# Cached window rows through on-chip slots in the last layer, and five smaller edits to a planned hybrid trunk kernel

## The chip, the cores and the metric

One core of a Trainium2 chip runs the whole program in one launch. Time is device microseconds of that core, lower is better. The kernel before takes 2428.99 us (median of 3 runs, 2427.99 to 2431.45).

## The reference

One inference step through four layers, A (gated short convolution), B (native sparse attention), C (RG-LRU recurrence) and A again, for 1024 prompt tokens and 8 x 4 sample tokens, width 1024, in f32. Beside the two results it returns new states; one of them is the sliding-window cache of the samples, a plain shift of the old one by four rows.

```python
def short_conv_mixer(x, buf, w_in, conv_w, w_out):
    h, b_gate, c_gate, z = jnp.split(x @ w_in, 4, axis=-1)
    conv, new_buf = causal_dwconv(c_gate * h, buf, conv_w)
    return (jax.nn.silu(z) * b_gate * conv) @ w_out, new_buf
...
x <- LayerNorm(ALPHA * x + mixer(x))
...
# nsa_win_sample: (8 samples, 512 rows, k and v, 2 heads, 64)
win = jnp.concatenate([win_buf, win_new], axis=1)   # the last 512 rows are returned
```

So rows 4 to 511 of each sample's cache, 508 rows of 1 KB (520,192 bytes), are returned unchanged as rows 0 to 507, and only the last four rows are computed (in layer B).

## The kernel before

Tokens lie in the free dimension, features in partitions: 1056 tokens as three pieces of 352 (`TC`), 1024 features as eight tiles of 128. A product in f32 is three products of split halves (`split` makes a high part by a cast on ScalarE and a low part by a subtraction on VectorE or GpSimd), so one piece of one output tile is a group of 24 matmuls in `dense`, and one weight tile (512 KB, loaded into `ws`, split into `w`) serves three such groups.

Every call is recorded (`Rec`), not issued: `Rec.lay` then plays a list schedule with a cost for each operation, a bus for the transfers and due times, over rings of tile slots (`big` 18 slots of 8.25 KB, `w` 3, `ws` 4 or 5, `c` 8 or 9 of one piece each, PSUM `mm` 5 and `aux` 3), and the order that it finds is the order on TensorE, VectorE, ScalarE and GpSimd. All instructions so recorded have line L310. The order of the transfers on SP, the queue that issues nearly all of them, is set by the framework beneath; SP issues them one by one, each when what it waits for is there, and each also waits for the transfer eight before it.

The first A layer carries side work (`compress`): 64 gathers of 1 MB of the paged cache by GpSimd, summed on GpSimd and VectorE, and written back to DRAM as `raw` (128 stores). It is shared over the layer's 96 steps (`share`): `RATE` side steps for each step. What remains is done at the layer's end. After the side work the layer's last carried rows `SC` are transposed on TensorE and stored.

In layer A a step (w, j) is a weight tile and a piece. For output tile c = 0 the pieces are outermost (three weights for j = 0, then for j = 1, then j = 2), so that the layer can begin while the LayerNorm of the layer before is still at work on the later pieces; that LayerNorm reloads what it needs by `c<-xc` and `c<-dd`. From c = 1 on each weight serves its three pieces in a row.

The old window rows are copied from DRAM to DRAM by eight transfers written in layer C (`gate_out`, one for each c). Nothing that they read depends on the program before them.

In layer B (`b_project`) the tiles of keys and values leave PSUM by a ScalarE copy into a slot of ring `c` (`kv`), one for each of 9 token tiles, from which rows are stored and keys transposed (`put_k`). `kl1` holds the low parts of the keys of group 1, by a transfer.

Stages of the profiled execution, in us from the span's start: first layer A 0 to 414, its output product to 540, projections of B to 690, sample attention to 861, prompt attention to 1455, output of B to 1560, C to 1850 and its output to 1935, the last A 1947 to 2301, its output to the end.

Of the kernel before, what the change touches and what calls it, by code (L numbers as in the profile page):

```python
# [240 lines left out]
class Rec:  # L241
# [136 lines left out]
    def lay(self):  # L378
        ops = self.ops
        for o in ops:  # L380
            o.weak -= o.deps
            o.left, o.ready, o.outs, o.follow = len(o.deps) + len(o.weak), 0.0, [], []
        for o in ops:
            for d in o.deps:
                d.outs.append(o)
            for d in o.weak:
                d.follow.append(o)
        free = {e: 0.0 for e in self.ENGINES}
        pend = {e: [] for e in self.ENGINES}
        able = {e: [] for e in self.ENGINES}  # L390
        num = {id(o): i for i, o in enumerate(ops)}
        parked = {}
        for r in self.rings:
            r.next = 0
            r.free = [0.0] * (r.n - len(r.held))
            for t in r.held:
                if not t.keep and not t.left:
                    r.free.append(0.0)

        def admit(o):  # L400

            for t in o.takes:
                if t.ring.next != t.seq or not t.ring.free:
                    parked[id(t.ring), t.seq] = o
                    return
            for t in o.takes:
                r = t.ring
                r.free.sort()
                o.ready = max(o.ready, r.free.pop(0))
                r.next += 1  # L410
            heapq.heappush(pend[o.eng], (o.ready, num[id(o)], o))
            for t in o.takes:
                wake(t.ring)

        def wake(r):
            o = parked.get((id(r), r.next))
            if o is not None and r.free:
                del parked[id(r), r.next]
                admit(o)
        for o in ops:  # L420
            if not o.left:
                admit(o)
        order, bus, table = [], 0.0, None
        while True:
            best = None
            for e in self.ENGINES:
                if able[e]:
                    s = free[e]
                elif pend[e]:
                    s = max(free[e], pend[e][0][0])  # L430
                else:
                    continue
                if best is None or s < best[0]:
                    best = (s, e)
            if best is None:
                break
            s, e = best
            while pend[e] and pend[e][0][0] <= s:
                _, i, o = heapq.heappop(pend[e])
                heapq.heappush(able[e], (o.due, i, o))  # L440
            o = heapq.heappop(able[e])[2]
            cost = o.cost
            if o.func is not None:
                f = o.func == AF.Sqrt
                if table is not f:
                    cost += 1283
                table = f
            if e == "SP":
                free[e] = s + 100
                bus = max(bus, s + 100) + o.size / 360  # L450
                o.end = bus + 2000
            else:
                free[e] = o.end = s + cost
                if o.size:
                    bus = max(bus, o.end) + o.size / 360
                    o.end = bus + 2000
            order.append(o)
            o.start = s
            for k in o.follow:
                k.ready = max(k.ready, s + .01)  # L460
                k.left -= 1
                if not k.left:
                    admit(k)
            for k in o.outs:
                lat = 0 if o.size and e == "POOL" else self.LAT.get((e, k.eng), 100)
                k.ready = max(k.ready, o.end + lat)
                k.left -= 1
                if not k.left:
                    admit(k)
            for t in o.tiles:  # L470
                t.left -= 1
                t.end = max(t.end, o.end + 150)
                if not t.left and not t.keep:
                    t.ring.free.append(t.end)
                    wake(t.ring)
        if len(order) != len(ops):
            done = {id(o) for o in order}
            stuck = [(o.eng, o.due, [t.name for t in o.takes], [t.ring.tag for t in o.takes]) for o in ops if id(o) not in done]
            raise RuntimeError(f"{len(stuck)} steps cannot start: {stuck[:12]}")
        return order  # L480
# [18 lines left out]
class Trunk:  # L499
# [447 lines left out]
    def layer_a(self, pm, a, X, lp, side=None, nxt=()):  # L947
        nc, io = self.nc, self.io
        stt = nc.vector.scalar_tensor_tensor
        win = io["a_w_in"][a]  # L950
        U = [None] * NCH
        SC = lp.tile([P, NCH, 36 if self.later else 18], F32, name="SC")
        todo = [(w, c) for c in range(NCH) for w in (0, 2, 3, 1)]
        wkey = lambda x: ("a", a) + x
# [12 lines left out]
        for c in range(NCH):  # L967
            g = self.wsl(1074)
# [5 lines left out]
            def step(w, j):  # L974
# [7 lines left out]
                if w == 0:  # L982
                    hs[j] = self.ct(TC)
                    nc.scalar.copy(hs[j], ps)
                elif w == 2:
                    nc.vector.tensor_mul(g[:, 2 + j * TC:2 + j * TC + np_], ps[:, 0:np_], hs[j][:, 0:np_])
                    if j == 2:
                        nc.vector.tensor_mul(gs[:, :, 2:6], ps[:, 320:352].rearrange("p (b t) -> p b t", t=4),
                                             hs[j][:, 320:352].rearrange("p (b t) -> p b t", t=4))
                elif w == 3:  # L990
                    th[j] = self.ct(TC)
                    nc.scalar.activation(th[j], ps, AF.Tanh, scale=0.5)
                    stt(out=th[j], in0=th[j], scalar=1.0, in1=ps, op0=ALU.add, op1=ALU.mult)
                else:
                    u = th[j]
                    stt(out=u, in0=ps, scalar=0.5, in1=u, op0=ALU.mult, op1=ALU.mult)
                    n = TC if j < 2 else 368
                    cv = self.aux(pm)[:, 0:n]
                    o = j * TC
                    nc.scalar.activation(cv, g[:, o:o + n], AF.Copy, scale=self.par(c, R_CA + 3 * a))  # L1000
                    for k in (1, 2):
                        stt(out=cv, in0=g[:, o + k:o + k + n], scalar=self.par(c, R_CA + 3 * a + k), in1=cv, op0=ALU.mult, op1=ALU.add)
                    parts = [(0, np_, cv[:, 0:np_])]
                    if j == 2:
                        parts.append((320, 352, cv[:, 320:368].rearrange("p (b t) -> p b t", t=6)[:, :, 2:6]))
                    for a0, b0, v in parts:
                        uv, uh, ul = u[:, a0:b0], *(U[c][:, i, o + a0:o + b0] for i in range(2))
                        if a0:
                            uv, uh, ul = (q.rearrange("p (b t) -> p b t", t=4) for q in (uv, uh, ul))
                        nc.vector.tensor_mul(v, uv, v)  # L1010
                        self.split(uh, ul, v, "act", "dve")
            U[c] = self.view2(self.big(F32R))
            if c == 0:
                seq = [(w, j) for j in range(3) for w in (0, 2, 3)] + [(1, j) for j in range(3)]
# [63 lines left out]
    def layer_c(self, pm, X, lp):  # L1078
        nc, io = self.nc, self.io
# [103 lines left out]
        def gate_out(c):  # L1183
            h2, i = H[c // 2], c % 2
# [3 lines left out]
            for j in range(3):  # L1188
# [5 lines left out]
                stt(out=th, in0=th, scalar=1.0, in1=ps, op0=ALU.add, op1=ALU.mult)  # L1194
                stt(out=th, in0=th, scalar=0.5, in1=h2[:, i, sl], op0=ALU.mult, op1=ALU.mult, wk=[("z", c)])
                self.split(u[:, 0, sl], u[:, 1, sl], th, "act", "pool")

            nc.sync.dma_start(win_s[c, 0:508, :], cache[c, 4:512, :], rk=[("z", c)])
        UC, GT, WA, H = {}, {}, {}, {}
        win_s = io["o_nsa_win_sample"][0].rearrange("b t c g d -> b t (c g d)")  # L1200
        cache = io["cache_nsa_win"][0].rearrange("b t c g d -> b t (c g d)")
        for x in ORDER_C.split():
            c = int(x[1])
            if x[0] == "u":
# [170 lines left out]
    def b_project(self, pm, X, bs, ds):  # L1375
        nc, io = self.nc, self.io
# [24 lines left out]
        def put_k(br, ps, g0, n):  # L1401


            for g in range(2):
                kd = K[br]
                r0, r1 = slice(64 * g, 64 * g + 64), slice(64 - 64 * g, 128 - 64 * g)
                sl = slice(g0, g0 + n)
# [10 lines left out]
        for half in range(2):  # L1418
# [8 lines left out]
            for g4 in ((0, 1, 2) if half == 0 else (2, 0, 1)):  # L1427
                tts = range(4 * g4, min(4 * g4 + 4, 9))
                kn = []
                if half == 1 and g4 == 0:  # L1430
                    side = self.decode_prepare(pm, q2, self.decode_gates(pm, GS, ds), KN, VN, ds)
                for tt in tts:
# [7 lines left out]
                            nc.tensor.matmul(ps, a, b, start=n == 0, stop=n == 23)  # L1440
                            n += 1
                    next(side, None)
                    kv = self.ct(nw)
                    if half == 0:
                        nc.scalar.copy(kv, ps)
                    else:
# [759 lines left out]
FOFF = 7  # L2206
OUT0, OUTD, OUT1, OUTE = 119.07, 2.4, 114, 0.993
OUTS = ((0, 0), (0, 1), (1, 0), (1, 1))
RATE = 0.7
GAHEAD = 3  # L2210
ORDER_C = "u101 u001 u12 u02 u2 g0 u5 z0 u3 g1 u4 g2 z1 z2 g3 u6 g4 u7 g5 z4 z3 g6 z6 z5 g7 z7"
NLO = (((2, 5, 6, 7), (3, 4, 6), (0, 5)), ((6, 7), (0, 5, 7), (2, 7)), ((2, 4, 6, 7), (1, 2, 6), (0, 1, 2, 3, 6, 7)))
# [14 lines left out]
TAILV = 39  # L2227
VLO = 0b10010010
SEL0 = 1
SELT = (3, 9, 18)  # L2230
DSH = dict(sel=7.1, kin=-11.8, begin=-11.6, keys=2.2, score=-10.9, turn=30.4, pv=-26.1, vin=-88.9, first=-37.1, vals=-23.0,
       fin=17.8, fold=-41.1, weights=-59.0, exps=-96.3)
DN = 3, 3, 3, 1
# [189 lines left out]
```

## Time and profile before

| | before |
|---|---|
| median of 3 runs | 2428.99 us |
| the profiled execution's own time | 2425.75 us |
| its span | 2423.7 us |
| TensorE busy in the span | 2305.6 us (95%) |
| VectorE, ScalarE, GpSimd busy | 1583.6, 1203.7, 959.3 us |
| bytes moved | 320.34 MB, 132 GB/s over the span |

TensorE is the long engine. A time is predicted against the profiled execution's own 2425.75 us; the median lies 3.24 us above that. An engine's idle time is read with what ended it, and a transfer engine's load with the DMA share of a stretch, which is the mean over the core's 16 DMA engines.

### The profile page before, as it was taken

How to read it: one execution, taken by the hardware profiler on the slowest of the kernel's cores; microseconds unless marked ns; L12 is line 12 of the kernel's file. 1: busy time of each engine (PE TensorE's matmuls, PEld its weight loads, DVE VectorE, ACT ScalarE, POOL GpSimd, SP SyncE). 2: the span in 40 equal slices, each digit the busy share in tenths (PEclk: the TensorE clock that was granted, in tenths of full speed). 3: DMA queues.
4: the chain of work that ended last, by engine and by line, in shares of the span. 5: the costliest groups of instructions: out<-in, count | busy, mean ns of one | idle time of the engine just before them, and what ended most of it. 6: DMA issues, size and time to landing. Idle time of an engine off the chain costs nothing. (4 is left out here: it accounts for less than half of the span.)

```text
span 2423.7 us, 41400 instructions
## 1 busy us (share of the span) xinstructions
PE 2305.6 (95%) x14801; PEld 2234.8 (92%) x14801; DVE 1583.6 (65%) x3686; ACT 1203.7 (50%) x2757; POOL 959.3 (40%) x1070
## 2 busy tenths in 40 slices
PE   8999997997989989999999999989999999999996
PEld 8999997996888879999999989989999999999996
DVE  5786875575358877777777777787765753433336
ACT  3211111234438878888888883487863442222233
POOL 3454543213137765565555552333463320000131
PEclk9999999997999999999999999999999999999998
DMA  7999988347356752111111234331113321111112
GB/s 260 351 350 338 321 291 281 98 151 245 104 175 230 247 201 56 33 47 43 47 48 41 78 123 124 117 103 53 53 47 118 99 67 53 44 44 53 35 46 72
DMA packets 334642, 320.34 MB, mean 132 GB/s; under 512 B 19462, under 2 KB 301542, under 8 KB 324964
## 3 DMA queue, kind: packets, MB, share of 16 engines
q1 hardware_dynamic: 325220, 250.58, 33.4%
q0 software_dynamic: 9216, 67.11, 7.4%
q8 instruction: 117, 1.92, 0.3%
q14 instruction: 89, 0.73, 0.1%
HBM read 237.31 MB, written 84.48 MB: 133 GB/s over the span
## 5 line engine op out<-in xcount | busy, mean ns | idle before, releaser
L310 PE MATMUL mm<-x,w 128*128 128x352 f32 x5760 | 948.9, 326 | 29.6 <-DVE ws L310 10.3
L310 PEld LDWEIGHTS mm<-x,w 128*128 128x128 f32 x5760 | 936.4, 190 | 36.6 <-DVE w L310 7.6
L310 PE MATMUL mm<-big,w 128*128 128x352 f32 x2208 | 375.4, 325 | 1.0 <-ACT c L310 1.0
L310 PEld LDWEIGHTS mm<-big,w 128*128 128x128 f32 x2208 | 357.2, 189 | 2.8 <-ACT c L310 1.3
L310 POOL TENSOR_TENSOR w<-ws,w 128x1024 fp32r<-128x1024 f32 (+1 forms) x43 | 104.8, 2438 | 445.8 <-ACT w L310 426.7
L1968 DVE TENSOR_TENSOR c<-T,c 128x512 fp32r<-128x512 f32 (+1 forms) x320 | 204.7, 648 | 49.3 <-ACT c L1964 44.9
L1964 ACT CAST c<-T 128x512 fp32r<-128x512 f32 (+1 forms) x320 | 174.3, 551 | 59.3 <-PE T L1960 37.7
L310 ACT CAST w<-ws 128x1024 fp32r<-128x1024 f32 (+2 forms) x116 | 120.3, 1038 | 163.3 <-PE mm L310 119.4
L641 PE MATMUL D<-x,w 128*128 128x352 f32 x1008 | 195.5, 330 | 2.2 <-DVE big L2095 2.2
L1870 PE MATMUL A<-big 128*128 128x320 f32 (+11 forms) x832 | 181.5, 334 | 3.4 <-DVE ast L1895 1.6
L1975 PE MATMUL O<-c,big 128*128 128x256 f32 x1056 | 180.4, 291 | 0.5 <-ACT c L1964 0.2
L310 POOL TENSOR_TENSOR big<-big,ws 128x1024 f32<-128x1024 f32 (+1 forms) x38 | 89.6, 2358 | 199.0 <-DMA big<-in_cache_nsa_kv,idx 103.9
L641 PEld LDWEIGHTS D<-x,w 128*128 128x128 f32 x1008 | 159.8, 188 | 5.7 <-DVE big L2095 3.5
L310 DVE TENSOR_TENSOR big<-big 128x256 f32<-128x256 f32 (+3 forms) x204 | 150.5, 758 | 21.7 <-POOL big L310 20.3
L310 DVE TENSOR_TENSOR w<-ws,w 128x1024 fp32r<-128x1024 f32 (+2 forms) x73 | 93.9, 1286 | 105.6 <-ACT w L310 104.8
L310 ACT CAST big<-aux 128x352 fp32r<-128x352 f32 (+3 forms) x116 | 45.4, 399 | 229.9 <-DVE aux L310 160.6
L1975 PEld LDWEIGHTS O<-c,big 128*128 128x128 f32 x1056 | 147.2, 189 | 2.5 <-DVE c L1968 0.7
L1928 POOL TENSOR_SCALAR pr<-pr,G,ast 128x32 f32<-128x32 f32 (+6 forms) x192 | 125.6, 668 | 47.1 <-DVE ast L1939 41.3
L1870 PEld LDWEIGHTS A<-big 128*128 128x128 f32 x832 | 134.3, 193 | 10.0 <-PE A L1870 2.2
L310 ACT ACTIVATE aux<-ws,PT 128x352 f32<-128x352 f32 (+2 forms) x72 | 42.7, 593 | 172.5 <-DVE ws L310 167.9
L1924 ACT ACTIVATE pr<-pr,ast 128x32 f32<-128x32 f32 (+6 forms) x192 | 118.4, 619 | 18.3 <-DVE ast L1895 17.4
L310 DVE SCALAR_TENSOR_TENSOR c<-c,mm 128x352 f32<-128x352 f32 x125 | 64.1, 515 | 92.3 <-ACT c L310 54.6
(286 smaller groups left out, 4032.7 us busy)
## 6 DMA issues: line engine op xcount, KB each, us to landing
ws<-in_a_w_in SPq DMA_DIRECT2D x64, 512.0 KB
raw<-big SPq DMA_DIRECT2D x128, 256.0 KB
big<-raw SPq DMA_DIRECT2D x128, 256.0 KB
c<-dd SPq DMA_DIRECT2D x48, 176.0 KB
xs<-x SPq DMA_DIRECT2D x24, 352.0 KB
x<-xs SPq DMA_DIRECT2D x8, 1056.0 KB
ws<-in_a_w_out SPq DMA_DIRECT2D x16, 512.0 KB
ws<-in_c_w_in SPq DMA_DIRECT2D x16, 512.0 KB
```

What stands on the lines that cost most here:

```text
L310: getattr(real, name)(*[f(x) for x in a], **{q: f(x) for q, x in k.items()})
L641: self.nc.tensor.matmul(ps, a, b, start=n == 0, stop=n == 23 and last)
L1870: nc.tensor.matmul(o, q[:, hl, i * P:(i + 1) * P], k, start=m == 0, stop=m == 1)
L1924: nc.scalar.activation(S[:, a:a + m], S[:, a:a + m], AF.Exp, bias=st[:, k:k + 1], scale=-1.0, accum_out=st[:, 3 + k:4 + k])
L1928: nc.gpsimd.tensor_scalar(S[:, a:a + m], S[:, a:a + m], G[:, i, 16 * k + h:16 * k + h + 1], st[:, 6 + k:7 + k], op0=ALU.mult, op1=ALU.mult)
L1964: nc.scalar.copy(x["H"][:, 0:n], x["tp"][:, 0:n])
L1968: nc.vector.tensor_sub(x["L"][:, 0:n], x["tp"][:, 0:n], x["H"][:, 0:n].bitcast(F32))
L1975: nc.tensor.matmul(O, v, M[:, y * P:(y + 2) * P], start=done[0] == 0, stop=done[0] == total - 1)
```

## The change

Six edits. (1) `Rec.lay` now counts 400 ns instead of 100 ns for a transfer's issue on SP and 330 instead of 360 bytes per ns for the bus. (2) The eight DRAM to DRAM copies in layer C are gone. In the last layer A (the only one with `side is None`) the loop over c loads two samples' 508 rows into a `big` slot for c = 0 to 3, as 127 partitions of four rows, and stores them in the next c. (3) `put_k` treats group 1 first. (4) `kv` lies in a quarter of a `big` slot instead of a `c` slot. (5) `RATE` goes from 0.7 to 0.75. (6) `SELT`, two step numbers at which the sample attention does its selection, go from 3 and 9 to 5 and 10.

```diff
             if e == "SP":
-                free[e] = s + 100
-                bus = max(bus, s + 100) + o.size / 360
+                free[e] = s + 400
+                bus = max(bus, s + 400) + o.size / 330
                 o.end = bus + 2000
             else:
                 free[e] = o.end = s + cost
                 if o.size:
-                    bus = max(bus, o.end) + o.size / 360
+                    bus = max(bus, o.end) + o.size / 330
...
         win = io["a_w_in"][a]
         U = [None] * NCH
+        win_s, win_c = (io[x][0].rearrange("b t c g d -> b t (c g d)") for x in ("o_nsa_win_sample", "cache_nsa_win"))
...
+            if side is None and c < 5:
+
+                if c:
+                    for i in range(2):
+                        nc.sync.dma_start(win_s[2 * c - 2 + i, 0:508, :].rearrange("(p t) f -> p t f", t=4), keep[:, i])
+                if c < 4:
+                    keep = self.big()[0:127, 0:2048].rearrange("p (b t f) -> p b t f", b=2, t=4)
+                    for i in range(2):
+                        nc.sync.dma_start(keep[:, i], win_c[2 * c + i, 4:512, :].rearrange("(p t) f -> p t f", t=4))
             U[c] = self.view2(self.big(F32R))
...
-
-            nc.sync.dma_start(win_s[c, 0:508, :], cache[c, 4:512, :], rk=[("z", c)])
...
-            for g in range(2):
+            for g in (1, 0):
                 kd = K[br]
...
                 kn = []
+                four = self.big()
...
-                    kv = self.ct(nw)
+                    kv = four[:, len(kn) * nw:(len(kn) + 1) * nw]
...
-RATE = 0.7
+RATE = 0.75
...
-SELT = (3, 9, 18)
+SELT = (5, 10, 18)
```

The edits move instructions in three places.

SP at the start of the last layer A (`ws<-in_a_w_in` is a weight tile; `c<-xc` and `c<-dd` are reloads for the LayerNorm of layer C, the five in a row those for its third piece; the lines with `127x1024` are the new loads and stores):

```order
+L310 DMA big<-in_cache_nsa_win 127x1024 x2
+L310 DMA c<-xc 128x352
+L310 DMA c<-dd 128x352
+L310 DMA c<-xc 128x352
+L310 DMA out_nsa_win_sample<-big 127x1024 x2
+L310 DMA big<-in_cache_nsa_win 127x1024
+L310 DMA ws<-in_a_w_in 128x8x128
+L310 DMA big<-in_cache_nsa_win 127x1024
+L310 DMA out_nsa_win_sample<-big 127x1024 x2
 L310 DMA c<-dd 128x352 x5
-L310 DMA ws<-in_a_w_in 128x8x128 x28
+L310 DMA ws<-in_a_w_in 128x8x128 x6
```

Two loads now stand ahead of the last reloads for the second piece, and eight new transfers in all ahead of those for the third. After the six weights come two loads and two stores, four weights, two loads and two stores, and then the other weights without a break; the weights stood in one row of 28 before.

TensorE at the end of the first layer A (`mm<-x,w` are its own groups, `aux<-idf,SC` the transposes of the carried rows, `mm<-big,w` the output product):

```order
 L310 MATMUL mm<-x,w 128x352 x2226
-L310 MATMUL aux<-idf,SC 18x128 x8
-L310 MATMUL mm<-big,w 128x352 x36
+L310 MATMUL mm<-big,w 128x352 x90
+L310 MATMUL aux<-idf,SC 18x128 x4
+L310 MATMUL mm<-big,w 128x352 x6
+L310 MATMUL aux<-idf,SC 18x128 x4
+L310 MATMUL mm<-big,w 128x352 x30
```

Ninety matmuls of the output product now stand ahead of the transposes that came first.

ScalarE in the projections of B (`COPY big<-mm` and `COPY c<-mm` take keys and values out of PSUM, `CAST big<-ws` splits a weight tile that has to be loaded first):

```order
+L310 COPY big<-mm 128x384 x4
 L310 CAST x<-c 128x352
 L310 ACTIVATE c<-c,PT 128x352 x2
 L310 CAST x<-c 128x352 x2
 L310 CAST big<-ws 128x1024
-L310 COPY c<-mm 128x384
-L310 ACTIVATE c<-c,PT 128x352
-L310 COPY c<-mm 128x384
```

Four copies out of PSUM stand ahead of the cast that they stood behind.

## Rows read from the trace of the kernel before

**Rows 1.** The page, queue of the gathers: packets, MB, share of 16 engines' span.
```profile
q0 software_dynamic: 9216, 67.11, 7.4%
```

**Rows 2.** Windows of 50 us: engines' busy time (count), TensorE's clock, DMA share, GB/s.
```profile
50.00:100.00 50.00, 50.00 (x314) 50.00 (x313) 35.27 (x50) 11.77 (x19) 25.11 (x15) 1.00 1.04 351
...
400.00:450.00 50.00, 33.84 (x195) 32.03 (x195) 30.55 (x56) 10.99 (x20) 12.65 (x9) 0.86 0.67 220
...
550.00:600.00 50.00, 36.07 (x169) 31.56 (x170) 27.91 (x51) 23.98 (x46) 19.85 (x19) 0.78 0.76 255
...
700.00:750.00 50.00, 47.02 (x302) 41.84 (x303) 39.88 (x116) 32.78 (x66) 30.80 (x32) 0.91 0.64 211
```

**Rows 3.** Window of the last layer A, same columns.
```profile
1950.00:2300.00 350.00, 350.00 (x2181) 350.00 (x2180) 133.00 (x252) 81.81 (x144) 24.46 (x19) 1.00 0.18 50
```

**Rows 4.** Tile `out_nsa_win_sample`: issue times (ns, min/median/max), first and last start.
```profile
L310 SPq DMA_DIRECT2D out_nsa_win_sample<-in_cache_nsa_win x8: 534/694/1307, 25.2 to 226.0; - x8
```

**Rows 5.** Waits of TensorE from 0 to 414 us: total us, times, longest.
```profile
PE mm L310 <- DVE ws L310: 10.3, 4, 4.5
```

**Rows 6.** Timeline of TensorE at the first layer's end: start, us, instruction [idle <-releaser].
```profile
402.05 11.85 PE L310 MATMUL mm<-x,w 128*128 128x352 f32 x72 [2.02 <-DVE ws L310]
426.22 1.02 PE L310 MATMUL aux<-idf,SC 128*18 128x128 f32 x4 [12.33 <-DVE big L310]
429.06 1.02 PE L310 MATMUL aux<-idf,SC 128*18 128x128 f32 x4 [1.82 <-DVE big L310]
```

**Rows 7.** Timeline of TensorE in B's projections and at the sample attention's start.
```profile
553.19 2.29 PE L310 MATMUL aux<-ones_m,big 128*128 128x1 f32 x10 [4.10 <-DVE big L310]
555.34 6.87 PE L310 MATMUL mm<-w,x 128*128 128x384 f32 x30
...
580.11 2.29 PE L310 MATMUL mm<-w,x 128*128 128x384 f32 x6 [8.67 <-ACT c L310]
...
702.98 0.66 PE L310 MATMUL aux<-idf,sel 128*128 128x128 f32 x2 [7.35 <-DMA sel<-kcd]
```

**Rows 8.** Timeline of ScalarE before the second of these.
```profile
578.63 1.04 ACT L310 CAST big<-ws 128x1024 fp32r<-128x1024 f32 x1 [2.58 <-DMA ws<-in_b_w_in]
```

**Rows 9.** DMA from 1957 to 1964 us: packets by size, queue (packets, MB, share), issues.
```profile
DMA packets 2080, 1.05 MB, mean 150 GB/s; under 512 B 32, under 2 KB 2080, under 8 KB 2080
...
ws<-in_a_w_in SPq DMA_DIRECT2D x2, 512.0 KB
```

**Rows 10.** DMA from 1833.2 to 1835.81 us, same columns.
```profile
DMA packets 130, 0.25 MB, mean 94 GB/s; under 512 B 24, under 2 KB 94, under 8 KB 130
...
q1 hardware_dynamic: 130, 0.25, 36.3%
...
out_lru_conv_sample<-ws SPq DMA_DIRECT2D x1, 96.0 KB
out_lru_h_sample<-ws SPq DMA_DIRECT2D x1, 32.0 KB
out_lru_conv_prompt<-ws SPq DMA_DIRECT2D x1, 12.0 KB
out_lru_h_prompt<-ws SPq DMA_DIRECT2D x1, 4.0 KB
```

**Rows 11.** Timeline of SP at the last layer's start.
```profile
1924.78 0.65 SPq L310 DMA_DIRECT2D c<-xc  x1
1926.93 0.32 SPq L310 DMA_DIRECT2D c<-dd  x1
...
1935.00 5.81 SPq L310 DMA_DIRECT2D c<-dd  x5
1957.67 277.40 SPq L310 DMA_DIRECT2D ws<-in_a_w_in  x28
```

**Rows 12.** The chain that ended last, at the last layer's start.
```profile
1924.78 5.06 DMA c<-xc
...
1946.91 354.78 PE mm L310 x2208
```

More of the change, by code (lines that the diff above doesn't have):

```diff
@@ L1196, in gate_out @@
                 self.split(u[:, 0, sl], u[:, 1, sl], th, "act", "pool")
-            nc.sync.dma_start(win_s[c, 0:508, :], cache[c, 4:512, :], rk=[("z", c)])
         UC, GT, WA, H = {}, {}, {}, {}
-        win_s = io["o_nsa_win_sample"][0].rearrange("b t c g d -> b t (c g d)")
-        cache = io["cache_nsa_win"][0].rearrange("b t c g d -> b t (c g d)")
         for x in ORDER_C.split():
```

## The prediction

> **What bounds the kernel now.** I read the windows first. In the last layer A TensorE is busy for all of 350 us at full clock, with the DMA engines at 18% [rows 3]; there the matmuls are the bound, and anything that delays a weight or a reload adds to the end one for one. In the first layer A it is the other way round: from 50 to 100 us the DMA share is 1.04 at 351 GB/s [rows 2], and TensorE waits 10.3 us in four pieces for VectorE's sums that stand behind late transfers [rows 5]. Next the timeline of TensorE, where the idle times before the prompt attention are to be seen: 12.33 and 1.82 us at the first layer's end, before the transposes of SC [rows 6]; 4.10 and 8.67 us in B's projections and 7.35 us at the sample attention's start [rows 7]. After each the windows show TensorE below full clock: mean 0.86, 0.78 and 0.91 over 50 us [rows 2], a mixture of its levels 2.4 and 1.2 GHz. Last I read the transfers at the start of the last layer A, because the change puts new ones there: the chain that ended last runs through a `c<-xc` of 5.06 us and then into 354.78 us of matmuls without a break [rows 12].
>
> **What it gives early.** The eight copies are not where the code has them. They read nothing that the program makes, and they are issued between 25.2 and 226.0 us [rows 4], in the saturated stretch. Each reads and writes 520,192 bytes, so eight are 8.3 MB or 24 us of traffic at 351 GB/s, half of it in each direction; with them gone, weights, gathers and stores come up to that much earlier. Of the 10.3 us I give back 6. At the layer's end, 90 matmuls of the output product now stand ahead of the transposes; at 11.85 us for 72 [rows 6] they are 14.8 us, as much as the 14.15 us of idle time they cover, if their own inputs are there. I give back 12, and 4 of the 7 us that the clock of 0.86 costs in 50 us. In B's projections 12 more matmuls ahead of `aux<-ones_m` are 2.7 us (30 take 6.87 [rows 7]) of the 4.10. The 8.67 us wait is for ScalarE, which stood for 2.58 us before a cast whose weight was not there until 578.63 [rows 8]; the copies out of PSUM now come before that cast, and I give back 3. With 2 us of clock that is 8. The start of the sample attention waits for a transfer that is issued a little earlier; of 7.35 and of the 4.5 us that the clock of 0.91 costs I give back 4. Sum: 22 + 8 + 4 = 34 us. The bounds: 8, if only half of the cover at the first layer's end holds, and 45, if the first layer's idle time, its clock and B's 12.8 us vanish almost whole. The other edits (planner costs, `SELT`, group order of `put_k`, `kv` in a `big` slot) show in the order only through these places; the prompt attention's and the last product's order stays, and I take the rest as nothing, within 5 us.
>
> **What the new transfers cost.** This is the large term and the trace has no transfer of 127 partitions. Its price is bounded by 16 engines and by one: 520,192 bytes are 1.5 us at 351 GB/s, and on one engine, at 351 / (16 x 1.04) = 21.1 GB/s [rows 2], 24.7 us. Which is nearer is read from the small packets. Each share of a transfer ends with one packet under 512 B. Two weight loads of 128 partitions have 32 of them [rows 9], 16 each. Four stores that run nearly by themselves, of 96, 32, 12 and 4 KB in rows of 4 KB, are 24, 8, 3 and 1 rows; their 36 packets of 4 KB are there (130 less 94), and 24 small ones [rows 10]. Sixteen for each would make 64, one for each row up to sixteen 3 + 16 + 1 + 8 = 28. It is 24 = 3 + 12 + 1 + 8: the 24 rows went in 12 equal shares. So a transfer is cut in as many equal shares as divide its rows, up to 16; 127 is a prime, and the share that fits is one. I take one engine, 25 us for each load and each store. The ends of this price: 22 us at the gathers' rate (67.11 MB in 7.4% of 16 engines' 2423.7 us [rows 1] are 23.4 GB/s) and 31.5 at that of the scattered stores (0.25 MB in 36.3% of 16 x 2.61 us [rows 10] are 16.5 GB/s).
>
> The Trainium skill, "DMA: Bandwidth & Descriptors", section "Why a DMA increments its semaphore by 16 and not by 1", gives the rule behind this: a transfer issued by SP runs on the largest number of engines up to 16 that divides the slowest dimension of both sides, and it names 127 partitions as a case of one engine, the lowest-numbered. The count of 24 agrees. By the opposite reading, 16 shares whatever the shape, the sum below would lose its large term and end near 2395 us.
>
> Sixteen transfers of 25 us on one engine are 400 us, against 355 us of matmuls that they were put beside. They do not run behind them, for three reasons. A weight or a reload goes over all 16 engines, so its last share stands behind every copy issued before it. A store reads the slot that its load fills, so SP waits at the store until the load has landed, and issues nothing behind it. And the order on SP puts them ahead of urgent transfers. Step by step, from 1924.5 us on the time axis of before:
>
> First, two loads, then `c<-xc`: it lands at about 1977 rather than 1930 [rows 11, 12], so TensorE stands for some 45 us. Then two stores, two loads and two stores more, with a weight between, before the five `c<-dd` that were issued at 1935.00 and are needed for the third piece of c = 0. Eight copies on one engine end near 1924.5 + 200, so the reloads land about 187 us late; some 10 us of that is slack (an estimate: the first two pieces have six groups, 23 us, begun at 1924 with 3 to 4 us of waits between, so their end is near 1951; the reloads landed at 1941). These two stalls together: 177 us.
>
> Then six weights, the last issued as soon as `w` tiles come free, about 2150 on the delayed axis. Behind it two loads (to 2200), at whose end the second store is issued; the eleventh weight comes after that and its last share lands behind both stores, near 2252, ready at 2257. TensorE, at 11.5 us for a weight (three groups of 24, by the 354.78 us for 2208 matmuls), needs it at 2230: 27 us. Then four weights and the last four copies: the fifteenth weight is ready 100 us after the eleventh, TensorE has 46 us of work: 54 us. After that weights come one after another again.
>
> Sum of the stalls 177 + 27 + 54 = 258 us. Four long idle times, each followed by a spell at the lower clock; by the mean clock of 0.86 and 0.78 [rows 2], 7 us for one in the first window and 11 for two in the second, that is 6 each, 24. Total: 2425.75 - 34 + 258 + 24 = 2674, and 3.24 above it for the median: 2677 us. At 22 us for a copy the stalls are 153 + 15 + 42 = 210, at 31.5 us 229 + 53 + 80 = 362; so 2632 to 2784, and with the bounds of the gain 2620 to 2800 for this case.
>
> **The rivals.** The copies are spread over the engines after all (the lowering splits a long contiguous row otherwise, as it did with the copies of before). Then each takes 1.5 us in a stage with 18% DMA share, SP's waits for a landing are some 3 us, the reload chain loses up to 5, and the 34 us of the early stages remain: 2395, between 2384 and 2425. For it speaks only that those were cut into sixteen; against it the count of small packets. It decides on the number of shares: at eight or more the copies pass beside the matmuls, below four they don't. This is the case on the other side.
>
> One engine for each, but not the same one. Then pairs run side by side, and before the five `c<-dd` stand three rounds of 25 us (two loads, two stores with the next two loads, two stores): they land some 60 us late, 50 after the slack; the later weights add 0 to 10, the clock 12: 2425.75 - 34 + 50 + 5 + 12 + 3.24 = 2462. No row shows on which engines shares run, so nothing speaks for it but that nothing excludes it.
>
> The Trainium skill, in the section named above, excludes it: the engines used are the lowest-numbered ones, so a single share is always on the same one. No run here shows the engine's number.
>
> The gain in the early stages fails: the gathers go on at their own pace and `SC` is late however the matmuls stand. With one-engine copies that is 2700, inside the first case.
>
> **How the numbers follow.** One engine, always the same: 0.85, 2677 us. One engine each, changing: 0.07, 2462. Spread: 0.07, 2395. Something that evens out: 0.01. A difference under 0.2% is no more than a measurement of this kernel can tell from none. Slower by more: 0.92; same 0.01; faster 0.07. The likeliest case alone holds 2620 to 2800 nine times in ten; the range goes down to 2500, for a case in which part of the stalls overlaps, and up to 2790.
>
> **What would show it.** In the trace of the changed kernel: the 127-row stores and loads with a small packet each instead of 16, and a DMA share of about 0.06 while they run; TensorE idle for tens of us near the last layer's start with a reload as releaser, twice, and then twice with a weight's split behind a late load; a last layer of some 600 us instead of 355. SP's waits there named by the loads of `in_cache_nsa_win`. Early on, no wait of 12 us before the transposes of SC, and a first layer that ends some 10 to 20 us sooner. Wrong would be the forecast if the window of the last layer still shows TensorE at 100%; then the copies were spread, and only the early terms count.

## The result, and the profile after

The changed kernel takes 2604.11 us (median of 4 runs, 2602.43 to 2605.89), the kernel before 2428.61 in the same comparison: a ratio of 1.072, 95% interval 1.0702 to 1.0739. It is slower by 175.5 us. The forecast was 2677 us, with 2500 to 2790 as the range: the direction and the mechanism came out, the size was 73 us too large.

The page of the changed kernel first (profiled execution 2603.26 us): its span, busy times, and TensorE's busy share and clock in 40 slices of 65 us.

```profile
span 2601.5 us, 41376 instructions
...
PE 2309.2 (89%) x14801; PEld 2236.4 (86%) x14801; DVE 1591.3 (61%) x3686; ACT 1201.8 (46%) x2757; POOL 957.9 (37%) x1070
...
PE   8999998989998999999999999999942197499996
...
PEclk9999999999999999999999999999976598799998
```

TensorE does the same work in the same busy time; all that is added is idle, and it lies in the slices from 1890 us on, which was the stretch without a wait [rows 3]. The waits of TensorE from 1880 to 2400 us (total, times, longest):

```profile
PE mm L310 <- ACT c L310: 156.4, 3, 103.3
PE mm L310 <- DVE ws L310: 34.9, 1, 34.9
PE mm L310 <- DVE w L310: 1.4, 1, 1.4
```

In order of time the four long ones are 34.92, 103.29, 17.07 and 36.07 us, 191.4 together. ScalarE and VectorE are named because they prepare what TensorE reads. They themselves waited for transfers: from 1900 to 2270 us the first of the four ends with VectorE's wait for a reload, the last two with ScalarE's waits for weights.

```profile
DVE ws L310 <- DMA c<-xc: 35.9, 1, 35.9
ACT w L310 <- DMA ws<-in_a_w_in: 89.1, 2, 54.0
```

For the longest the profile names no releaser: VectorE goes on with the LayerNorm at 2066.28, right after the copies ahead of the five `c<-dd` are through (below). SP's timeline shows how late all these were issued (start, duration of the issue):

```profile
1901.04 2.89 SPq L310 DMA_DIRECT2D big<-in_cache_nsa_win  x2
1904.10 20.11 SPq L310 DMA_DIRECT2D c<-xc  x1
1924.30 8.14 SPq L310 DMA_DIRECT2D c<-dd  x1
1932.53 1.15 SPq L310 DMA_DIRECT2D c<-xc  x1
1933.77 18.18 SPq L310 DMA_DIRECT2D out_nsa_win_sample<-big  x2
1952.04 19.63 SPq L310 DMA_DIRECT2D big<-in_cache_nsa_win  x1
1971.77 19.60 SPq L310 DMA_DIRECT2D ws<-in_a_w_in  x1
1991.41 10.21 SPq L310 DMA_DIRECT2D big<-in_cache_nsa_win  x1
2005.07 27.44 SPq L310 DMA_DIRECT2D out_nsa_win_sample<-big  x2
2032.60 23.81 SPq L310 DMA_DIRECT2D c<-dd  x5
2078.72 12.07 SPq L310 DMA_DIRECT2D ws<-in_a_w_in  x6
2090.84 10.16 SPq L310 DMA_DIRECT2D big<-in_cache_nsa_win  x2
```

In before the five `c<-dd` were issued 10 us after the first `c<-xc` shown there [rows 11]; here it is 128 us, and the rest of their lateness is in the queue behind the copies. A window of 20 us in which nothing but copies runs shows what a copy is: DMA from 2010 to 2030 us (packets by size; queue with packets, MB, share of 16 engines; issues).

```profile
DMA packets 130, 0.53 MB, mean 26 GB/s; under 512 B 1, under 2 KB 1, under 8 KB 130
...
q1 hardware_dynamic: 130, 0.53, 6.4%
...
out_nsa_win_sample<-big SPq DMA_DIRECT2D x2, 508.0 KB
```

The last load before the five `c<-dd` runs to 2026 in this window and the first of the two stores after it. A share of 6.4% is one engine of sixteen. It takes 129 packets of 4 KB in 20 us, 155 ns each, so that a copy of 127 takes 19.7 us; and there is one small packet where a transfer of 128 rows has sixteen [rows 9]. Whether two copies have the same engine is seen right after the first two loads, both issued by 1903.93. DMA from 1905 to 1923 us:

```profile
DMA packets 116, 0.48 MB, mean 26 GB/s; under 512 B 0, under 2 KB 0, under 8 KB 116
...
q1 hardware_dynamic: 116, 0.48, 6.4%
```

Two transfers are out and one engine works. The reload issued behind them lands at 1944.66, 40.56 us after its issue began (the chain that ended last), which is two copies of 19.7. The eight copies ahead of the five `c<-dd` end one after another, each with its small packet, the first at 1924.1 and the eighth at 2065.4.

### The profile page after: what moved, and what is told of

Its sections match the earlier page's. It is cut to its first block, busy times and chain, and to the rows that moved or that the text cites. A ratio compares the mean times of both kernels' runs of the same rounds, so it can differ in the third digit from the quotient of the medians.

```text
span 2601.5 us, 41376 instructions
## 1 busy us (share of the span) xinstructions
PE 2309.2 (89%) x14801; PEld 2236.4 (86%) x14801; DVE 1591.3 (61%) x3686; ACT 1201.8 (46%) x2757; POOL 957.9 (37%) x1070
## 5 line engine op out<-in xcount | busy, mean ns | idle before, releaser
L310 DVE TENSOR_TENSOR big<-big 128x256 f32<-128x256 f32 (+3 forms) x204 | 173.8, 872 | 19.2 <-POOL big L310 17.3
L310 POOL TENSOR_TENSOR big<-big 128x512 fp32r<-128x512 f32 (+2 forms) x74 | 86.4, 1184 | 96.2 <-DVE big L310 72.3
L310 DVE TENSOR_TENSOR c<-c 128x352 f32<-128x352 f32 (+1 forms) x85 | 52.7, 654 | 109.3 <-issue 108.0
```

What stands on the lines that cost most here:

```text
L310: getattr(real, name)(*[f(x) for x in a], **{q: f(x) for q, x in k.items()})
```

## The experiments

There are two things to explain: four long waits late, and a gain early. Each run below is against the kernel before on the same chip; the time is the median. Where fewer rows are copied, the rest is left out of the output.

**More shares, nothing else.** Each copy as 128 rows of 4,064 bytes:

```diff
-   keep = self.big()[0:127, 0:2048].rearrange("p (b t f) -> p b t f", b=2, t=4)
+   keep = self.big()[:, 0:2032].rearrange("p (b e) -> p b e", b=2)
...
-   win_c[2 * c + i, 4:512, :].rearrange("(p t) f -> p t f", t=4)
+   win_c[2 * c + i, 4:512, :].rearrange("t f -> (t f)").rearrange("(p e) -> p e", p=128)
```

> The changed kernel with each copy of 520,192 bytes as 128 rows of 4,064 bytes instead of 127 of 4,096; the same instructions in the same order on every engine. Theory (a transfer of 127 rows is one share on one engine, and all that follows queues behind it): with sixteen shares a copy takes under 2 us, the four waits of 34.9, 103.3, 17.1 and 36.1 us in the last layer A go, and about 11 us of clock with them: 2604 - 191 - 11 = 2402 us, between 2396 and 2410. Rival (SP's standing at the stores and the place of the new transfers ahead of the reloads cost by themselves, whatever the number of shares): at least half of the 191 us stays, 2500 us or more.

2403.42 us, ratio 0.9904 (0.9884 to 0.9924). The waits of TensorE in the same stretch, 1880 to 2320 us, are now

```profile
PE mm L310 <- DVE w L310: 3.0, 1, 3.0
PE mm L310 <- DVE x L310: 0.4, 1, 0.4
```

and the SP rows are short, with the same transfers in the same order:

```profile
1895.21 1.01 SPq L310 DMA_DIRECT2D big<-in_cache_nsa_win  x2
1896.38 0.33 SPq L310 DMA_DIRECT2D c<-xc  x1
...
1900.10 1.62 SPq L310 DMA_DIRECT2D out_nsa_win_sample<-big  x2
...
1914.42 2.67 SPq L310 DMA_DIRECT2D c<-dd  x5
```

So 200 us hang on one row more, with the order on the four other engines the same throughout. That SP stands at a store until its load has landed, and that the copies are ahead of the reloads, costs some 3 us when a copy is short. The rival with 2500 us falls.

**Two shares.** Rows `[0:122]` of the 127 in loads and stores.

> The changed kernel, but only the first 122 of the 127 groups of four rows of each sample are loaded and stored (20 of its 508 cached rows are left out of the output); 122 has 2 as its largest divisor up to 16. Theory (equal shares): a copy takes 61 packets of 155 ns, 9.5 us instead of 19.7; the reloads for the third piece come 8 x 9.5 = 76 us late instead of 158, which with the 20 us that were slack at 158 makes 56 us of waits, the two later waits go, the clock costs 5: about 2402 + 61 = 2463 us, between 2445 and 2480. Rival (any number of rows not a multiple of 16 runs on one engine): 122 packets instead of 127, about 2595 us. Rival (spread over all engines but for 127 alone): 2402.

2463.48 us, ratio 1.0148 (1.0121 to 1.0176). Its waits in the last layer A:

```profile
PE mm L310 <- ACT c L310: 41.7, 1, 41.7
PE mm L310 <- DVE w L310: 16.7, 2, 16.5
```

58.4 us against 56 worked out, and the two later waits are gone. (In its last layer A the planner's order differs a little: a weight stands ahead of the second pair of loads.) DMA from 2028 to 2036 us, where copies alone run, has two small packets, two sixteenths of the engines and twice the rate:

```profile
DMA packets 105, 0.42 MB, mean 53 GB/s; under 512 B 2, under 2 KB 2, under 8 KB 105
...
q1 hardware_dynamic: 105, 0.42, 12.8%
```

Two engines took half the time of one, so it is the number of equal shares, and neither "127" nor "not a multiple of 16", that decides.

**Half the work for the one engine.** Loads of 127 rows, stores of `[0:16]`.

> The changed kernel, but of each loaded copy only 16 of 127 groups of rows are stored (the rest of the shifted cache is left out of the output); loads and order unchanged. SP still stands at each store until the 127-row load has landed, but the one engine has half of the work. Theory (the queue on the one engine decides): four loads of 19.7 us stand before the reloads, 79 us late instead of 158, less 20 of slack, 59 us; the later waits of 17 and 36 us lose 39 each and go; clock 6: about 2467 us, between 2450 and 2485. Rival (SP's standing at the stores decides): SP stands as long as before, the time stays above 2550.

2474.44 us, ratio 1.0193 (1.0167 to 1.0218), in the range of the queue and 7 us above its point:

```profile
PE mm L310 <- DVE ws L310: 64.4, 2, 35.2
PE mm L310 <- DVE w L310: 1.6, 2, 1.4
```

The first wait is as long as in the changed kernel, since the two loads ahead of the first reload are still there; what is gone is what the stores put into the queue. SP stood at the stores for the landing of the same loads, and the loss fell from about 200 us to 71.

**Fourteen shares.** Rows `[0:126]`, one execution.

> The changed kernel with 126 of the 127 groups of four rows loaded and stored (4 of a sample's 508 cached rows are left out of the output); the same instructions in the same order. 126 divides by 14. Theory (equal shares, as many as divide the rows): fourteen engines, 9 packets of 155 ns, 1.4 us a copy: within 5 us of the 128 rows, 2398 to 2408 us. Rival (whatever doesn't divide by 16 runs on few engines): above 2450 us.

2411.67 us, 4 us above the upper end. No wait of 3 us or more is left in its last layer. From 2005 to 2013 us two loads and two stores end, and there are 56 small packets, four times fourteen:

```profile
DMA packets 516, 1.88 MB, mean 236 GB/s; under 512 B 56, under 2 KB 56, under 8 KB 516
```

The time above the range is not from the copies. The transposes of SC start at 438.10 us here and at 430.32 with 128 rows, and the last layer A at 1907.7 and 1895.6, before any of these copies and with the same instructions in the same order; from there to the last group of matmuls the two take 485.6 and 484.3 us. In the five kernels that have the changed kernel's first layer the transposes start between 429.5 and 438.3 us, so single profiles of the same work differ there by up to 9 us.

**The other five edits, with the copies where they were.**

```diff
+            nc.sync.dma_start(win_s[c, 0:508, :], cache[c, 4:512, :], rk=[("z", c)])   # back in gate_out
-            if side is None and c < 5: ...                                             # layer_a
```

> The changed kernel with the eight copies from DRAM to DRAM back where they were (written in layer C) and no new ones: the other five edits alone. Theory: the 15 us less idle time in the projections of B and at the start of the sample attention come from the key and value tiles in a large slot and the order of the groups, and stay; the part of the first layer A, some 7 us, goes: about 2414 us, between 2406 and 2420. Rival (the early gain of 22 us comes from the removed copies): 2425 us or more. Rival (it comes wholly from the other edits): 2403 or less.

2390.99 us, ratio 0.9857 (0.9834 to 0.9879). I had taken 2406 to 2420; this is the rival by which the gain comes wholly from the other edits, and it is faster than with the copies moved in sixteen shares, by 12 us. The early gain is wholly that of the five other edits, and moving the copies takes a part of it back. Up to the start of the last layer A, TensorE, VectorE, ScalarE and GpSimd have the same instructions in the same order in both; what differs there is SP (in the last layer A the planner's order differs too). Without the eight copies SP's order in the first layer A is another (more stores of `raw` ahead of the weights), and the gathers end later. Tile `idx` with first and last gather, the kernel with 128 rows, then the one with the old copies:

```profile
L315 POOL DMA_INDIRECT big<-in_cache_nsa_kv,idx x64: 932/981/2195, 34.8 to 421.6; - x64
```

```profile
L315 POOL DMA_INDIRECT big<-in_cache_nsa_kv,idx x64: 933/1016/2197, 34.7 to 416.7; - x64
```

In the changed kernel it is 424.9 us, and with the copies alone moved 424.8 against 416.6 in before. Less traffic did not make the gathers quicker. That SP's order, which the framework chooses, made them later is argued from what differs, and was not tested by itself. It is also not all of the 12 us: the two profiled executions lie 7.7 us apart, 4.5 of it at the start of the last layer A and 3.3 in that layer.

**Which of the five.** On the kernel before, one edit at a time: the planner's costs; `RATE`; the key and value slots with the order of groups; and the copies moved as 128 rows.

```diff
e5: -  free[e] = s + 100 ... / 360     +  free[e] = s + 400 ... / 330
e6: -  RATE = 0.7                       +  RATE = 0.75
e7: -  kv = self.ct(nw)                 +  kv = four[:, len(kn) * nw:(len(kn) + 1) * nw]
    -  for g in range(2):               +  for g in (1, 0):
e8: the edit of the first experiment, and no other
```

> The kernel before with the planner's transfer costs alone changed (400 ns for an issue, 330 bytes per ns). In its order the 90 matmuls of the output product stand ahead of the transposes of SC, and two copies out of PSUM ahead of the cast in B. Theory (this edit gives the gain of the first layer A, and the slots of the key and value tiles that of B and of the sample attention): about 18 us less, 2411 us, between 2405 and 2418. Rival (the rate of the side work gives the first layer's gain): within 5 us of before.

> The kernel before with RATE 0.75 alone. The order at the first layer's end stays as before (the transposes of SC ahead of the output product). Theory of e5: the side work is bound by its transfers, so calling it earlier moves little: 2424 to 2432 us. Rival (the rate gives the first layer's gain): 2412 or less.

> The kernel before with the key and value tiles in a large slot and the other order of the groups in put_k, and nothing else. Theory of e5: the idle times of 4.10 and 8.67 us in B's projections and of 7.35 us at the sample attention's start lose the 15 us that they lost in the changed kernel: about 2412 us, between 2405 and 2419. Rival (these too came from the planner's costs): within 5 us of before.

> The kernel before with the copies moved to the last layer A as 128 rows of 4,064 bytes (sixteen shares), and nothing else. If the removal of the copies from the first layer A is worth what the prediction said (6 us of waits and some of the clock) it is faster, 2415 to 2422 us. If it costs as the fourth experiment says against the first (12 us more with the copies moved than with the old ones, five of them in the first layer A, where the order of the transfers on SP changes), it is slower, 2434 to 2442 us.

| alone on the kernel before | median us | ratio (95%) |
|---|---|---|
| planner's costs | 2407.49 | 0.9899 (0.9871 to 0.9927) |
| `RATE` 0.75 | 2421.95 | 0.9958 (0.9936 to 0.9980) |
| key and value slots, `put_k` | 2418.57 | 0.9947 (0.9930 to 0.9963) |
| copies as 128 rows | 2438.69 | 1.0036 (1.0021 to 1.0051) |

The planner's costs alone give 22.6 us, the slots 11.5, the rate 8.1, 42 in sum against 39 for all together (`SELT` was not run alone); moving the copies costs 8.6 even in the good shape. The rate is 2 us below its range, the other three lie in theirs. How two numbers in a planner give most of the 22 us is seen at the first layer's end, in the kernel with that edit alone (TensorE's timeline):

```profile
391.45 14.62 PE L310 MATMUL mm<-big,w 128*128 128x352 f32 x90
426.19 1.02 PE L310 MATMUL aux<-idf,SC 128*18 128x128 f32 x4 [20.12 <-DVE big L310]
```

The transposes of SC start at 426.19, as in before to 0.03 us [rows 6], and the wait ahead of them is longer, 20.12 instead of 12.33. But the 90 matmuls of the output product are already done, 14.6 us of work, and the second wait of 1.82 is gone: 16 us. A planner that believes in quick transfers puts the transposes first, where they block TensorE in order; one that believes in slower ones puts ready work ahead.

**Further along the same way.** The kernel of the fourth experiment with `RATE = 0.8`, and with 600 ns and 300 bytes per ns.

> The kernel of the fourth experiment (old copies, the five other edits) with RATE 0.8. If the wait of some 10 us before the transposes of SC is for side work that is called late, it is shorter by half and the time 2385 us; if the side work is bound by its transfers, 2388 to 2396 us, the same.

> The kernel of the fourth experiment with still slower transfers in the planner (600 ns for an issue, 300 bytes per ns). If the planner's gain comes from transfers that it had taken for quicker than they are, more of it is left: 2380 to 2388 us. If what it had was enough, 2388 to 2400 us.

2392.96 us (0.9853, 0.9816 to 0.9891), the same as with 0.75, but not because the side work is bound by its transfers: in its profile the last gather is issued at 409.3 us instead of 416.7 and the transposes start at 420.85 instead of 425.29. TensorE has lost this lead again by the start of the prompt attention; why is not settled. And 2416.19 us (0.9948, 0.9929 to 0.9968): slower costs than 400 and 330 are worse by some 25 us, with a wait of 30.08 us ahead of the transposes. Both expectations of the latter missed; more caution is not better, and why the plan comes out so is not settled.

The best version here is the fourth experiment's: the five other edits without the moved copies.

## Why the prediction was right, and where it was off

**One share on one engine: shown.** The share of 6.4%, the single small packet, the steps of time with the number of shares (1: 2604, 2: 2463, 14: 2412, 16: 2403 us). The count of small packets in before [rows 10] had said it. The Trainium skill, "DMA: Bandwidth & Descriptors", section "Why a DMA increments its semaphore by 16 and not by 1", gives the rule that a transfer runs on the largest number of engines up to 16 that divides its slowest dimension on both sides; the traces agree for 16, 14, 12, 2 and 1 shares. That a single share is always on the same engine is confirmed by the window from 1905 to 1923 us, in which two loads are out and one engine is busy; the rival with 2462 us falls. Of the prediction's reasons why the copies don't run behind the matmuls, the queue on the one engine carries most: with the stores cut to 16 rows SP still stood for the same loads, and 130 of the 200 us went.

**The price of a copy: mis-sized.** I took 25 us, with 22 as the lower end; it is 19.7, outside both ends. The price was taken from the saturated first layer [rows 2], where sixteen engines work at once on transfers of other shapes; alone with 4 KB packets one engine moves 26 GB/s. Which of the two differences makes it faster no run shows. By the prediction's own steps, with 19.7 us in place of 25, the stalls are 177 - 8 x 5.3 = 135 for the first two, 6 and 33 for the later ones, 174 in all; measured were 138, 17 and 36, 191. So the price takes 84 us off the 258, and the steps were 17 too short, 11 of them at the third wait. (Two slips of the prediction's sums change nothing: with 22 and 31.5 us a copy its terms give 2629 and 2781, not 2632 and 2784, and 2618 to 2807 with the bounds of the gain; with no early gain they give 2711, not 2700.)

**The clock: mis-sized.** From the first group of the last layer A to the end it is 499.6 us in before (2423.7 less 1924.1) and 699.9 after (2601.5 less 1901.6). Of the 200.3 more, 190 are waits (the 191.4, and the short one of 1.4, less the 2.4 us that before has there); 10 are left for the clock and all else, where I had 24.

**The early gain: mis-sized, and put down to the wrong edit.** The last layer A begins 22.5 us earlier, not 34. By places, from the rows of the changed kernel that answer to [rows 6, 7]:

```profile
433.66 1.02 PE L310 MATMUL aux<-idf,SC 128*18 128x128 f32 x4 [10.66 <-DVE big L310]
...
564.05 2.29 PE L310 MATMUL mm<-w,x 128*128 128x384 f32 x6 [5.39 <-ACT big L310]
...
680.03 0.41 PE L310 MATMUL aux<-idf,sel 128*128 128x128 f32 x2 [1.23 <-DMA sel<-kcd]
```

The transposes come 7.4 us later than in before, with 14.8 us of product done ahead of them and the second wait of 1.8 gone: 9 us of gain where I had 22 (by single profiles, which differ here by up to 9 us). So the sign "no wait of 12 us before the transposes" did not come: 10.66 us are left of it. VectorE was the reason, in its order of work:

```profile
427.67 1.22 DVE L310 TENSOR_TENSOR big<-big,ws 128x1024 f32<-128x1024 f32 x1 [3.76 <-DMA big<-in_cache_nsa_kv,idx]
...
433.08 0.52 DVE L310 TENSOR_TENSOR big<-aux,big 128x352 fp32r<-128x352 f32 x1 [2.54 <-ACT big L310]
```

It waits for the last gather, issued at 424.9, and what TensorE needs stands behind that. I had let the removed traffic bring the gathers forward; they came later (416.6 us in before). From there to the second row it is some 7 us (580.11 less 564.05, less the 9), to the third 7 more: 7 and 7 where I had 8 and 4. The step that failed is "weights, gathers and stores come up to that much earlier": the copies' removal gave nothing (8.6 us lost alone, 12 lost against the old copies), and the edits that I took as nothing outside the order gave the whole.

**How the misses add up.** Against the forecast the price took 84 us off, the steps came 17 longer, the clock and the rest 14 shorter, and the early gain was 11 smaller: 70 of the 73 us. The mechanism was right; that the misses partly cancel is luck.

**What the rival of spread copies said** was 2395 us; with 128 rows it is 2403, that case as it would have been, with 26 us gained instead of 34.

## What to carry to other kernels

Before a transfer from the SP queue is planned beside other work, look at its number of rows: what counts is in how many equal shares, up to 16, they can be cut. 127 rows, a prime, made one share, and every later transfer over all engines queued behind it. The same bytes as 128 rows of an unusual length took some 1.5 us a copy instead of 19.7 (two loads and two stores run within 6 us, 1990.5 to 1996.8, in that run). And when several edits come together, take the harmful one out alone: here five of the six were worth 39 us and the one in the title undid them five times over.

## What the runs showed of the hardware that was not expected

SP itself stands while it issues. Behind two loads of 127 packets for one engine the issue of a small reload lasted 20.11 us, and ended at 1924.21, as the first of the loads was through (its small packet is at 1924.1); with sixteen shares the same issue took 0.33 us. The later long issues do not end with a copy (the load issued at 1952.04 held SP until 1971.67, between two copies' ends at 1965.0 and 1984.7), so what SP stands for is not shown. A wait that the semaphores don't show can thus lie in the issue row itself. With two shares it was 8.26 us, in the timeline of SP of that run:

```profile
1904.23 1.02 SPq L310 DMA_DIRECT2D big<-in_cache_nsa_win  x2
1905.42 8.26 SPq L310 DMA_DIRECT2D c<-xc  x1
```

And one engine by itself moved 4 KB packets in 155 ns, 26 GB/s, a quarter more than the 21.1 GB/s of each in the saturated stretch of before.
